# Norm tiles, first memory values and queries in other buffers, a later turn for the third cross head, and whole rows in the last stores

## The chip, the core and the metric

One core of a Trainium2 chip runs the whole program: TensorE (PE) for matrix products, VectorE (DVE), ScalarE (ACT) and GpSimd (POOL) for the elementwise work, SyncE (SP) for issuing most of the transfers. The metric is the device time of one execution in microseconds (us), of which the median over several runs is taken.

## What is computed

One inference step of a two-layer encoder with 1024 features. Its tokens are 256 of a prompt and 32 of a sample, held side by side as 288 columns. Each layer is a mixing attention (another kind in each layer), a cross-attention of 4 heads into 256 memory tokens, and a gated feed-forward net; each of the three has an RMS norm in front and is added to the residual. A last norm gives the output.

```
def rmsnorm(x, g):
    y = xf * lax.rsqrt(jnp.mean(xf * xf, axis=-1, keepdims=True) + RMS_EPS)
    return (y * g)

def memory_attn(h, mk, mv, w_q, w_o):
    q = (h @ w_q).reshape(b, t, XA_HEADS, XA_HEAD_DIM)
    s = jnp.einsum('bqhd,bkhd->bhqk', q, mk) * (XA_HEAD_DIM ** -0.5)
    p = jax.nn.softmax(s, axis=-1)
    o = jnp.einsum('bhqk,bkhd->bqhd', p, mv)
    return o.reshape(b, t, D_MODEL) @ w_o
...
xp = xp + o @ w_out            # mixing
xp = xp + memory_attn(rmsnorm(xp, g_xattn), mk, mv, w_xq, w_xo)
xp = xp + swiglu(rmsnorm(xp, g_ffn), w_gate, w_up, w_down)
...
y_prompt = rmsnorm(xp, g_final); y_sample = rmsnorm(xs, g_final)
```

## The kernel before

**Matrix products.** The residual lies transposed in eight blocks `x[0..7]` of 128 features by 288 tokens. Every product with a weight is made in three terms: operand and weight are each split into a rounded part and a rest (`hh`, `hl` of the activations, `hi`, `lo` of the weights), and PE multiplies hh by hi, hl by hi and hh by lo. A **unit** (L185) is one weight tile of 128 x 1024 (512 KB): SP issues its load into `st`, ACT casts `hi` from it (L162), DVE subtracts to get `lo` (L163), and PE takes 24 matmuls of 288 columns over it, eight blocks of three. `project` (L200) is one unit, after which `tick` (L239) lets each running attention do one step; an attention that says `wait(n)` sits out n units. So the matmuls of the attentions stand in a row between units of weights, in an order that the program fixes.

**Split and norm of the next stage.** At the end of a mixing attention `out_project` adds each finished block `op` to `x[m]` (L399, DVE) and hands it to `Next`, which makes `hh` (L327, ACT) and `hl` (L330, DVE: scale and subtract) and gives the block to `Norm.add`: ACT squares it (`sq`, L269), and the squares are summed (`ssq`): the second by DVE (L280), the third to seventh by POOL, the eighth by DVE (both L282). `Norm.wide` then splits the sum into `qh` (ACT, L403) and `ql` (DVE, L404), PE takes the mean with two matmuls `nrm`, and eight DVE operations (L286 to L294) turn it into `rstd`. These two `nrm` matmuls stand 27 matmuls behind the first `pj` of the queries' projection, which uses the unscaled `hh` and `hl`; `rstd` is multiplied in afterwards (L715, with the sample's part in L717).

**Buffers.** `tok` tiles (66 of them, tag "t") hold nearly everything of one block: `hh`, `hl`, `sq`, `ssq`, the attention outputs `oh` and `ol`. Other tiles are `wk` tags: "w" (8 tiles), "w2" (4 tiles three times as wide), "bi" and "vn" (5 each). A tile that is allocated takes a buffer that was freed, and its first writer waits for the last users of that buffer. The engine waits in its own queue, so all that stands behind it waits too.

**Cross-attention.** `head(hd)` takes the scores `xs`, the softmax on DVE and ACT (`st` the row maxima and sums, `xe` the exponentials; L443 scales `xe` by 1/sum), waits a unit, transposes (`xt`, four plain float32 matmuls, L731), splits into `xw`, waits a unit, and multiplies by the memory values `vh`, `vl` into `xo`. The memory's last values are made in between by `memory.steps` (`mv`, then `vl` by POOL, and POOL's stores of `mv`). `sample` does the same for the 32 sample tokens (`xss`, `xst`, `xso`, `xsp`). PSUM has 4 banks "pj" for units and 4 banks "at" for attentions.

**End.** The last norm's mean is taken by 12 small matmuls, 8 DVE operations on six columns follow, PE transposes the scaled residual, and DVE and ACT scale it out of PSUM into `yo` (L1132, L1134). The sample's 32 rows are transposed as four strips of 256 columns, so that they lie in 128 partitions. SP issues four stores: the sample in blocks 4 x 32 x 256 (128 KB), the first 128 rows in two halves (256 KB each, rows of 2 KB) and the next 128 rows (512 KB, rows of 4 KB).

Of the kernel before, what the change touches and what calls it, by code (L numbers as in the profile page):

```python
# [15 lines left out]
P = 128  # L16
NT = 288
# [9 lines left out]
def encoder_step(ctx: ExitStack, tc: tile.TileContext, a):  # L27
# [17 lines left out]
    def name(s):  # L45
        cnt[0] += 1
        return f"{s}{cnt[0]}"

    def tok(s, dt=F32):
        return tk.tile([P, 320], dt, tag="t", name=name(s))[:, 0:NT]  # L50

    def work(s):
        return wk.tile([P, 512], F32, tag="w", name=name(s))

    def work2(s, dt=F32):
        return wk.tile([P, 768], dt, tag="w2", bufs=4, name=name(s))
# [120 lines left out]
    def together(ins):  # L177

        tc.keep_in_program_order(ins)
# [79 lines left out]
    class Norm:  # L259

        def __init__(self, n=NT, hurry=False):
            self.n, self.acc, self.parts, self.hurry = n, [None, None], 0, hurry
            self.tiles = [0, 128] + ([n - 128] if n > 256 else [])

        def add(self, xb, eng=None):
            q = tok("sq")
            S.activation(q[:, :self.n], xb[:, :self.n], AF.Square)  # L269
            self.parts += 1  # L270
            eng = eng or (V if self.parts == KT else G)
            i = int(self.parts == KT and self.hurry)
            if self.acc[i] is None:
                self.acc[i] = q
                return
            s = tok("ssq")
            b, c = self.acc[i][:, :self.n], q[:, :self.n]
            if self.parts == 2:

                V.scalar_tensor_tensor(s[:, :self.n], b, EPS * KT, c, op0=ALU.add, op1=ALU.add)  # L280
            else:
                eng.tensor_tensor(s[:, :self.n], b, c, ALU.add)  # L282
            self.acc[i] = s
# [11 lines left out]

        def wide(self):

            hi, lo = split(self.acc[0], tok("qh", F32R), tok("ql", F32R), V)
            p = att("nrm")[:, :self.n]
            mm(p, meanr, hi, True, False)  # L300
            mm(p, meanr, lo, False, True)
            r = big.tile([P, NT], F32, tag="rstd", bufs=2, name=name("rstd"))
            self.rsqrt(p, tok("y"), tok("nt"), r)
            return r

        def columns(self, between=None, bank=att):
# [26 lines left out]
    class Next:  # L333


        def __init__(self, gi):
            self.gi, self.norm, self.h, self.waiting = gi, Norm(hurry=gi == 8), ([], []), []

        def block(self, m, start=False):
            g = gain[:, self.gi * KT + m:self.gi * KT + m + 1]  # L340
# [61 lines left out]
    def split(t, hi, lo, eng=G):  # L402
        S.copy(hi, t)  # L403
        eng.tensor_tensor(lo, t, hi.bitcast(F32), ALU.subtract)  # L404
        return hi, lo
# [217 lines left out]
    class Memory:  # L623
# [31 lines left out]
        def step(self):  # L655
            i, l = self.i, self.l
            self.i += 1
            if i < 8:
                p = project(a["w_xk"][l, i], self.h, NP)
                t = tok("mk")  # L660
                V.tensor_tensor(t[:, 0:NP], p[:, 0:NP], memrow, ALU.mult)
                store(a["mkT"][l, i], t[:, 0:NP])
                self.k.append(split(t[:, 0:NP], tok("kh", F32R)[:, 0:NP], tok("kl", F32R)[:, 0:NP]))
            else:

                i -= 8
                heads, n, u, last = (2, 2, i, 3) if i < 4 else (1, 4, i % 2, 1)
                if u == 0:
                    self.p = [acc("mv") for _ in range(heads)]
                w = unit(a["w_xv"][l, i])  # L670
                m = 256 * heads
                for c in range(n):
                    k = n * u + c
                    b = slice(c * m, c * m + m)
                    for t in range(2):
                        d, tb = self.p[t][:, 0:m] if heads == 2 else self.p[0][:, 256 * t:256 * t + 256], slice(128 * t, 128 * t + 128)
                        first = k == 0 and (heads == 2 or t == 0)
                        mm(d, self.h[0][k][:, tb], w[0][:, b], first, False)
                        mm(d, self.h[0][k][:, tb], w[1][:, b], False, False)
                        mm(d, self.h[1][k][:, tb], w[0][:, b], False, k == KT - 1)  # L680
                    if c == 1 and fine[0]:
                        tick(0.5)
                tick(0.5 if fine[0] else 1)
                if u == last:
                    for hd in range(heads):
                        for t in range(2):
                            d = self.p[t][:, 256 * hd:256 * hd + 256] if heads == 2 else self.p[0][:, 256 * t:256 * t + 256]
                            f = hd if heads == 2 else i // 2
                            v = tok("mv")
                            V.tensor_scalar(v[:, 0:NP], d, memcol[:, t:t + 1], None, op0=ALU.mult)  # L690
                            store(a["mv"][l, t, :, f * 256:f * 256 + 256], v[:, 0:NP])
                            self.v[t, f] = split(v[:, 0:NP], tok("vh", F32R)[:, 0:NP], tok("vl", F32R)[:, 0:NP], V if f == 3 else G)


    def cross(layer, cur, memory, nxt):
# [8 lines left out]

        def room(s, i):

            if i < 10:
                return wk.tile([P, NP], F32R, tag=("vn", "bi")[i % 2], bufs=5, name=name(s))
            if i % 2 == 0:
                room.pair = wk.tile([P, 2 * NP], F32R, tag="w2", bufs=4, name=name(s))  # L710
            return room.pair[:, (i % 2) * NP:(i % 2) * NP + NP]

        def evac(b, p):
            t = tok("xq")[:, 0:NP]
# [4 lines left out]
        def head(hd):  # L719
            yield 1  # L720
            s = att("xs")
            for t in range(2):
                for f in range(2):
                    mm3s(s[:, 256 * t:256 * t + 256], q[2 * hd + f], slice(128 * t, 128 * t + 128), memory.k[2 * hd + f], slice(0, NP), f == 0, f == 1)
            e = work("xe")
            softmax(s, [(0, 256), (256, 512)], None, e)
            yield from wait(1)
            tt = att("xt")
            for kt in range(2):
                for t in (1, 0):  # L730
                    i = T.transpose(tt[:, 256 * kt + 128 * t:256 * kt + 128 * t + 128], e[:, 256 * t + 128 * kt:256 * t + 128 * kt + 128], ident)  # L731
                    together(i)
            w = [wk.tile([P, 512], F32R, tag="w", name=name("xw")) for _ in range(2)]
            split_o(tt, w[0], w[1])
            yield from wait(1)
            po = att("xo")
            for f in range(2):
                for kt in range(2):
                    mm3s(po[:, 256 * f:256 * f + 256], memory.v[kt, hd], slice(128 * f, 128 * f + 128), w, slice(256 * kt, 256 * kt + 256), kt == 0, kt == 1)
            for f in range(2):  # L740
                split_o(po[:, 256 * f:256 * f + 256], o[0][2 * hd + f][:, 0:256], o[1][2 * hd + f][:, 0:256])
# [364 lines left out]
        cur = nxt  # L1106


    banks = [[acc("yt"), acc("yt")], [acc("yt"), acc("yt")]]
    strips = att("yt")  # L1110

    def turn(t, m):

        if t < 2:
            return T.transpose(banks[t][m // 4][:, P * (m % 4):P * (m % 4) + P], cur.h[0][m][:, P * t:P * t + P], ident)
        out = strips[NS * (m // 2):NS * (m // 2) + NS, P * (m % 2):P * (m % 2) + P]
        return mm(out, cur.h[0][m][:, P * t:NT], ident)

    def turn_early():
        for m in range(4):  # L1120
            turn(0, m)

    y = cur.norm.columns(turn_early)
    for t, m in [(2, m) for m in range(KT)] + [(0, m) for m in range(4, KT)] + [(1, m) for m in range(KT)]:
        not_before(turn(t, m), cur.norm.summed.ins)
    out = [wp.tile([P, 1024], F32, tag="st", bufs=4, name=name("yo")) for _ in range(3)]

    def read(eng, t, c0, c1):
        src, scale = (banks[t][c0 // 512] if t < 2 else strips), y[:, 2 * t:2 * t + 1]
        b = slice(c0 % 512, c0 % 512 + c1 - c0)  # L1130
        if eng is V:
            together(V.tensor_scalar(out[t][:, c0:c1], src[:, b], scale, None, op0=ALU.mult))  # L1132
        else:
            together(S.activation(out[t][:, c0:c1], src[:, b], AF.Copy, scale=scale))  # L1134


    read(V, 2, 0, 256)
    together(DMA.dma_start(a["y"][2 * P:NT].rearrange("q (s c) -> s q c", s=4), out[2][:, 0:256]))
    read(S, 0, 0, 256)
    read(V, 0, 256, 512)  # L1140
    together(DMA.dma_start(a["y"][0:P, 0:512], out[0][:, 0:512]))
    read(S, 0, 512, 768)
    read(V, 0, 768, 1024)
    together(DMA.dma_start(a["y"][0:P, 512:1024], out[0][:, 512:1024]))
    read(S, 1, 0, 512)
    read(V, 1, 512, 1024)
    together(DMA.dma_start(a["y"][P:2 * P], out[1]))


_OUTS = {  # L1150
# [80 lines left out]
```

## Time and profile before

| what | value |
|---|---|
| median of 3 runs | 946.23 us (946.20 to 946.56) |
| the profiled execution, its own time | 946.38 us |
| its span, first to last instruction | 944.7 us (1.7 us lie around it) |
| mean granted TensorE clock | 0.999 |
| PE, DVE, ACT, POOL busy | 98%, 63%, 51%, 24% of the span |
| chain of work that ended last, by engine | PE 95%, DVE 2%, ACT 1%, DMA 1% |
| one ACT cast `hi`, one DVE subtraction `lo` (means) | 1.050 us, 1.230 us |

The page gives the busy time of each engine, groups of instructions with the mean duration of one, and the chain of work that ended last. Behind it lie views of the trace: the waits of one engine, and the instructions of an engine in order of time, each with its start, its duration and what ended the idle time before it. A PE row's duration includes filling the array and writing out; consecutive matmuls overlap, so for PE the distance from start to start is what counts.

### The profile page before, as it was taken

The numbers are of one execution on the slowest core, as the hardware profiler recorded it, in microseconds if no ns is written. First come the engines' busy times: TensorE is split into PE (matmuls) and PEld (weight loads), VectorE is DVE, ScalarE is ACT, GpSimd is POOL, SyncE is SP. The second block draws the span as 40 slices with busy tenths as digits, with TensorE's granted clock in tenths as the row PEclk, the third lists the DMA queues.
The fourth block names the chain that finished last, engine by engine and source line by source line (L and its number), as shares of the span: only waits on it lengthen the run. The fifth ranks groups of instructions, "written<-read, shape, count | busy, mean of one in ns | idle before, by whom it ended". The sixth has DMA issues, their size and how long they took to land.

```text
span 944.7 us, 18787 instructions
## 1 busy us (share of the span) xinstructions
PE 930.4 (98%) x7350; PEld 899.2 (95%) x7350; DVE 599.1 (63%) x1145; ACT 485.9 (51%) x861; POOL 229.2 (24%) x347
## 2 busy tenths in 40 slices
PE   8999999999999999999999999999999999999996
PEld 8999999999999999999999999899999999999996
DVE  6795555886775555855486666668768655555442
ACT  6566876555554444444455555555546544444330
POOL 4341212201122222400026443322101322221010
PEclk9999999999999999999999999999999999999999
DMA  8675444553444544554556455444425544444431
GB/s 292 198 246 187 164 147 161 175 172 130 147 165 169 175 161 170 184 195 166 183 199 213 170 196 180 172 170 155 146 102 178 179 169 167 166 169 168 167 113 51
DMA packets 49629, 160.96 MB, mean 170 GB/s; under 512 B 7196, under 2 KB 8412, under 8 KB 49540
## 3 DMA queue, kind: packets, MB, share of 16 engines
q1 hardware_dynamic: 45348, 149.23, 46.3%
q0 software_dynamic: 3904, 10.04, 2.9%
q8 instruction: 58, 0.95, 0.4%
q10 hardware_dynamic: 288, 0.48, 0.2%
q14 instruction: 31, 0.25, 0.1%
HBM read 149.58 MB, written 10.15 MB: 169 GB/s over the span
## 4 chain that ended last, share of the span: by engine, by line
PE 95%; DVE 2%; ACT 1%; DMA 1%; issue 0%; POOL 0%; SPq 0%; DVEq 0%; ACTq 0%
PE pj L68 54%; PE dn L68 15%; PE op L68 10%; PE mv L68 5%; PE po L68 1%; PE sc L68 1%; PE zb L68 1%; PE xo L68 1%; PE xs L68 1%; DMA first<-w_first 1%; PE nrm L68 0%; PE xt L731 0%; PE xss L68 0%; PE os L68 0%; POOL ssq L282 0%
## 5 line engine op out<-in xcount | busy, mean ns | idle before, releaser
L162 ACT CAST hi<-st 128x1024 fp32r<-128x1024 f32 x257 | 268.9, 1050 | 287.7 <-issue 104.5
L68 PE MATMUL pj<-hh,hi 128*128 128x288 f32 (+1 forms) x1344 | 397.1, 295 | 0.0
L68 PE MATMUL pj<-hh,lo 128*128 128x288 f32 (+1 forms) x1344 | 394.1, 293 | 0.2 <-DVE lo L163 0.2
L68 PE MATMUL pj<-hl,hi 128*128 128x288 f32 (+1 forms) x1344 | 393.9, 293 | 0.0
L163 DVE TENSOR_TENSOR lo<-st,hi 128x1024 fp32r<-128x1024 f32 x257 | 316.0, 1230 | 80.2 <-PE dn L68 40.1
L68 PEld LDWEIGHTS pj<-hh,hi 128*128 128x128 f32 x1344 | 252.9, 188 | 5.3 <-issue 4.3
L68 PEld LDWEIGHTS pj<-hh,lo 128*128 128x128 f32 x1344 | 252.8, 188 | 0.6 <-DVE lo L163 0.6
L68 PEld LDWEIGHTS pj<-hl,hi 128*128 128x128 f32 x1344 | 252.9, 188 | 0.0
L68 PE MATMUL dn<-fh,hi 128*128 128x288 f32 x416 | 109.9, 294 | 0.0
L68 PE MATMUL dn<-fh,lo 128*128 128x288 f32 x352 | 103.4, 294 | 0.0
L68 PE MATMUL dn<-fl,hi 128*128 128x288 f32 x288 | 84.6, 294 | 0.0
L282 POOL TENSOR_TENSOR ssq<-ssq,sq 128x288 f32<-128x288 f32 (+1 forms) x35 | 37.3, 1066 | 185.7 <-ACT sq L269 151.1
L68 PE MATMUL op<-oh,hi 128*128 128x288 f32 x256 | 76.0, 298 | 0.0
L68 PE MATMUL op<-ol,hi 128*128 128x288 f32 x256 | 75.4, 295 | 0.0
L68 PE MATMUL op<-oh,lo 128*128 128x288 f32 x256 | 75.3, 295 | 0.0
L68 PEld LDWEIGHTS dn<-fh,hi 128*128 128x128 f32 x416 | 74.5, 188 | 0.0
L68 PEld LDWEIGHTS dn<-fh,lo 128*128 128x128 f32 x352 | 66.0, 188 | 0.0
L820 POOL TENSOR_TENSOR fl<-us,fh 128x288 fp32r<-128x288 f32 x36 | 33.2, 922 | 106.1 <-ACT fh L819 106.1
L816 POOL TENSOR_TENSOR gs<-gs,sg 128x288 f32<-128x288 f32 x44 | 39.3, 892 | 74.0 <-ACT sg L814 72.8
L815 DVE TENSOR_TENSOR us<-pj,rstd 128x288 f32<-128x288 f32 x44 | 20.1, 457 | 58.0 <-PE pj L68 58.0
L68 PEld LDWEIGHTS dn<-fl,hi 128*128 128x128 f32 x288 | 54.0, 188 | 0.0
L68 PEld LDWEIGHTS op<-oh,hi 128*128 128x128 f32 x256 | 47.9, 188 | 0.6
(282 smaller groups left out, 1215.8 us busy)
## 6 DMA issues: line engine op xcount, KB each, us to landing
st<-w_gate SPq DMA_DIRECT2D x44, 512.0 KB, 3.2
st<-w_up SPq DMA_DIRECT2D x44, 512.0 KB, 3.3
st<-w_down SPq DMA_DIRECT2D x44, 512.0 KB, 3.2
st<-w_c SPq DMA_DIRECT2D x24, 512.0 KB, 3.5
st<-w_ab SPq DMA_DIRECT2D x21, 512.0 KB, 4.3
st<-w_xk SPq DMA_DIRECT2D x16, 512.0 KB, 3.5
st<-w_xv SPq DMA_DIRECT2D x16, 512.0 KB, 3.3
st<-w_xq SPq DMA_DIRECT2D x16, 512.0 KB, 3.5
```

Source lines behind the costliest of these rows:

```text
L68: return T.matmul(out, lhsT, rhs, start=start, stop=stop, skip_group_check=True)
L162: a = S.copy(hi, st[:, c0:c1])
L163: b = V.tensor_tensor(lo, st[:, c0:c1], hi.bitcast(F32), ALU.subtract)
L282: eng.tensor_tensor(s[:, :self.n], b, c, ALU.add)
L815: V.tensor_tensor(us, pu[:, :NT], cur.r, ALU.mult)
L816: G.tensor_tensor(gs, gs, sg, ALU.mult)
L820: G.tensor_tensor(lo, us, hi.bitcast(F32), ALU.subtract)
```

## The change

It touches five things.

1. The norm in front of each cross-attention (`gi` 2 and 3) takes its tiles `sq`, `ssq`, `qh`, `ql`, `y`, `nt` from tag "w" through a new helper `spare`, where it took `tok` tiles.
2. The memory values `vh`, `vl` of the first head (`f == 0`) go to tag "bi" in place of `tok`.
3. The sixteen query tiles of the cross-attention: the first twelve lie three to a "w2" tile and the last four in "vn"; before, ten lay in "vn" and "bi" in turn and six two to a "w2" tile.
4. The third head (`hd == 2`) waits two units instead of one between its scores and its transposes.
5. At the end the sample's rows are transposed like the others into two banks, each half of a bank pair is read by DVE and ACT, and the stores are two of 256 KB, one of 512 KB and last one of 32 whole rows (128 KB).

```diff
+    def spare(s, dt=F32):
+        return wk.tile([P, NT], dt, tag="w", name=name(s))
...
-        def __init__(self, n=NT, hurry=False):
-            self.n, self.acc, self.parts, self.hurry = n, [None, None], 0, hurry
+        def __init__(self, n=NT, hurry=False, tile=tok):
+            self.n, self.acc, self.parts, self.hurry, self.tile = n, [None, None], 0, hurry, tile
...
-            q = tok("sq")
+            q = self.tile("sq")
...
-            s = tok("ssq")
+            s = self.tile("ssq")
...
-            hi, lo = split(self.acc[0], tok("qh", F32R), tok("ql", F32R), V)
+            hi, lo = split(self.acc[0], self.tile("qh", F32R), self.tile("ql", F32R), V)
...
-            self.rsqrt(p, tok("y"), tok("nt"), r)
+            self.rsqrt(p, self.tile("y"), self.tile("nt"), r)
...
-            self.gi, self.norm, self.h, self.waiting = gi, Norm(hurry=gi == 8), ([], []), []
+            self.gi, self.norm, self.h, self.waiting = gi, Norm(hurry=gi == 8, tile=spare if gi in (2, 3) else tok), ([], []), []
...
-                            self.v[t, f] = split(v[:, 0:NP], tok("vh", F32R)[:, 0:NP], tok("vl", F32R)[:, 0:NP], V if f == 3 else G)
+                            parts = [wk.tile([P, NP], F32R, tag="bi", bufs=5, name=name(s)) if f == 0 else tok(s, F32R)[:, 0:NP] for s in ("vh", "vl")]
+                            self.v[t, f] = split(v[:, 0:NP], *parts, V if f == 3 else G)
...
-            if i < 10:
-                return wk.tile([P, NP], F32R, tag=("vn", "bi")[i % 2], bufs=5, name=name(s))
-            if i % 2 == 0:
-                room.pair = wk.tile([P, 2 * NP], F32R, tag="w2", bufs=4, name=name(s))
-            return room.pair[:, (i % 2) * NP:(i % 2) * NP + NP]
+            if i > 11:
+                return wk.tile([P, NP], F32R, tag="vn", bufs=5, name=name(s))
+            if i % 3 == 0:
+                room.three = wk.tile([P, 3 * NP], F32R, tag="w2", bufs=4, name=name(s))
+            return room.three[:, (i % 3) * NP:(i % 3) * NP + NP]
...
-            yield from wait(1)
+            yield from wait(2 if hd == 2 else 1)
...
-    read(V, 2, 0, 256)
-    together(DMA.dma_start(a["y"][2 * P:NT].rearrange("q (s c) -> s q c", s=4), out[2][:, 0:256]))
-    read(S, 0, 0, 256)
-    read(V, 0, 256, 512)
-    together(DMA.dma_start(a["y"][0:P, 0:512], out[0][:, 0:512]))
-    read(S, 0, 512, 768)
-    read(V, 0, 768, 1024)
-    together(DMA.dma_start(a["y"][0:P, 512:1024], out[0][:, 512:1024]))
-    read(S, 1, 0, 512)
-    read(V, 1, 512, 1024)
-    together(DMA.dma_start(a["y"][P:2 * P], out[1]))
+    for c in (0, 512):
+        read(V, 0, c, c + 256)
+        read(S, 0, c + 256, c + 512)
+        together(DMA.dma_start(a["y"][0:P, c:c + 512], out[0][:, c:c + 512]))
+    for t in (1, 2):
+        read(V, t, 0, 512)
+        read(S, t, 512, 1024)
+        together(DMA.dma_start(a["y"][P * t:min(P * t + P, NT)], out[t][rows[t]]))
```

The order of the instructions on the engines moves with the buffers, since the buffers decide what waits for what. First place: POOL, at the end of layer 0's mixing attention, the five sums `ssq` of the norm. The brackets name the engines that a row waits for. Before:

```order
L282 TENSOR_TENSOR ssq_2276<-ssq_2261,sq_2274 128x288 [waits DVE_49,PE_49,Activation_49]
L282 TENSOR_TENSOR ssq_2316<-ssq_2276,sq_2314 128x288 [waits PE_49,Activation_49]
L282 TENSOR_TENSOR ssq_2356<-ssq_2316,sq_2354 128x288 [waits PE_49,Activation_49]
L282 TENSOR_TENSOR ssq_2396<-ssq_2356,sq_2394 128x288 [waits PE_49,Activation_49,Pool_49]
L282 TENSOR_TENSOR ssq_2436<-ssq_2396,sq_2434 128x288 [waits PE_49,Activation_49,Pool_49]
```

After:

```order
L285 TENSOR_TENSOR ssq_2276<-ssq_2261,sq_2274 128x288 [waits DVE_49,Activation_49]
L285 TENSOR_TENSOR ssq_2316<-ssq_2276,sq_2314 128x288 [waits Activation_49,Pool_49]
L285 TENSOR_TENSOR ssq_2356<-ssq_2316,sq_2354 128x288 [waits Activation_49,Pool_49]
L285 TENSOR_TENSOR ssq_2396<-ssq_2356,sq_2394 128x288 [waits Activation_49,Pool_49]
L285 TENSOR_TENSOR ssq_2436<-ssq_2396,sq_2434 128x288 [waits Activation_49,Pool_49]
```

The sums stand in the same order; none of them waits for PE any more.

Second place: DVE, the last blocks of the same out-projection up to the norm's `ql`. Before:

```order
L163 TENSOR_TENSOR lo_2609<-st_2606,hi_2608 128x1024
L330 SCALAR_TENSOR_TENSOR hl_2351<-x_80,x_78,hh_2350 128x288
L330 SCALAR_TENSOR_TENSOR hl_2391<-x_80,x_78,hh_2390 128x288
L399 TENSOR_TENSOR x_81<-x_81,op_2444 128x288
L330 SCALAR_TENSOR_TENSOR hl_2431<-x_81,x_78,hh_2430 128x288
L163 TENSOR_TENSOR lo_2647<-st_2644,hi_2646 128x1024
L330 SCALAR_TENSOR_TENSOR hl_2471<-x_81,x_78,hh_2470 128x288
L282 TENSOR_TENSOR ssq_2476<-ssq_2436,sq_2474 128x288
L404 TENSOR_TENSOR ql_2554<-ssq_2476,qh_2553 128x288
```

After:

```order
L403 TENSOR_TENSOR x_81<-x_81,op_2404 128x288
L166 TENSOR_TENSOR lo_2607<-st_2604,hi_2606 128x1024
L333 SCALAR_TENSOR_TENSOR hl_2431<-x_81,x_78,hh_2430 128x288
L403 TENSOR_TENSOR x_81<-x_81,op_2444 128x288
L166 TENSOR_TENSOR lo_2643<-st_2640,hi_2642 128x1024
L333 SCALAR_TENSOR_TENSOR hl_2471<-x_81,x_78,hh_2470 128x288
L285 TENSOR_TENSOR ssq_2476<-ssq_2436,sq_2474 128x288
L408 TENSOR_TENSOR ql_2554<-ssq_2476,qh_2553 128x288
```

The rests `hl` of the earlier blocks, three of which stood around the last add to `x`, now stand each behind its own block's add; behind the last add there remain one `lo` and one `hl` ahead of the last sum.

Third place: PE, the third cross head of layer 0. Here `pj` is a unit of the fourth head's queries, `xt` the third head's transposes, `mv` a unit of the memory values. Before:

```order
L68 MATMUL pj_3047<-hh_2242,hi_3043 128x288
L68 MATMUL pj_3047<-hl_2243,hi_3043 128x288
L731 MATMUL xt_3026<-ident,xe_2972 128x128 x4
L68 MATMUL pj_3047<-hh_2242,lo_3044 128x288
L68 MATMUL pj_3047<-hh_2255,hi_3043 128x288
```

After:

```order
L71 MATMUL pj_3032<-hl_2471,hi_3028 128x288
L71 MATMUL pj_3032<-hh_2470,lo_3029 128x288
L736 MATMUL xt_3057<-ident,xe_2965 128x128 x4
L71 MATMUL mv_3081<-hi_3084,hh_690 128x256
L71 MATMUL mv_3081<-lo_3085,hh_690 128x256
```

The transposes moved from the third place of a unit of 24 to behind its last matmul, and the twelve `xo` matmuls that belong to them from in front of the `mv` unit and the eight `xss` to behind these. Two other moves on PE: the second `nrm` matmul stands right behind the first, where three `pj` stood between, and head 0's `xt` right behind the eight `xss`, where four `pj` stood between. Layer 1 has the same moves, and PE's count of instructions is the same.

## Rows read from the trace of the kernel before

**Rows 1.** The page, busy time of each engine (share of the span), instructions

```profile
PE 930.4 (98%) x7350; PEld 899.2 (95%) x7350; DVE 599.1 (63%) x1145; ACT 485.9 (51%) x861; POOL 229.2 (24%) x347
```

**Rows 2.** PE's waits: line, releaser, us in total, times, longest

```profile
PE nrm L68 <- ACT qh L403: 2.5, 2, 1.2
PE xt L731 <- DVE xe L443: 1.9, 2, 1.0
```

**Rows 3.** PE in order of time, layer 0's norm: start, us, instruction, [idle before]

```profile
179.31 0.29 PE L68 MATMUL op<-oh,lo 128*128 128x288 f32 x1
...
182.86 0.30 PE L68 MATMUL pj<-hh,lo 128*128 128x288 f32 x1
184.40 0.40 PE L68 MATMUL nrm<-qh,meanr 128*128 128x288 f32 x1 [1.24 <-ACT qh L403]
```

**Rows 4.** POOL in order of time, the same stretch

```profile
176.85 1.88 POOL L282 TENSOR_TENSOR ssq<-ssq,sq 128x288 f32<-128x288 f32 x1 [6.62 <-PE op L68]
...
181.81 1.39 POOL L282 TENSOR_TENSOR ssq<-ssq,sq 128x288 f32<-128x288 f32 x1 [0.74 <-POOL ssq L282]
```

**Rows 5.** DVE in order of time, the same stretch

```profile
180.33 0.44 DVE L399 TENSOR_TENSOR x<-x,op 128x288 f32<-128x288 f32 x1
...
181.32 1.21 DVE L163 TENSOR_TENSOR lo<-st,hi 128x1024 fp32r<-128x1024 f32 x1
182.45 1.06 DVE L330 SCALAR_TENSOR_TENSOR hl<-x,x,hh 128x288 fp32r<-128x288 f32 x1
183.44 0.45 DVE L282 TENSOR_TENSOR ssq<-ssq,sq 128x288 f32<-128x288 f32 x1
```

**Rows 6.** All `hl` of this shape: count, ns min/median/max, first and last start

```profile
L330 DVE SCALAR_TENSOR_TENSOR hl<-x,x,hh x36: 505/514/1071, 7.6 to 726.4; 128x288 fp32r<-128x288 f32 x36
```

**Rows 7.** DVE in order of time, from the norm's mean to the queries

```profile
185.37 0.46 DVE L286 TENSOR_SCALAR y<-nrm 128x288 int32<-128x288 int32 x1 [0.53 <-PE nrm L68]
...
194.00 0.41 DVE L404 TENSOR_TENSOR ql<-xq,qh 128x256 fp32r<-128x256 f32 x1
```

**Rows 8.** PE in order of time, first head's scores and transposes

```profile
194.47 0.38 PE L68 MATMUL xs<-kh,ql 128*128 128x256 f32 x1
...
198.66 1.06 PE L68 MATMUL xss<-ca,xqs 128*32 128x256 f32 x8
199.65 0.40 PE L68 MATMUL pj<-hh,hi 128*128 128x288 f32 x1
199.89 0.29 PE L68 MATMUL pj<-hl,hi 128*128 128x288 f32 x1
200.02 0.29 PE L68 MATMUL pj<-hh,lo 128*128 128x288 f32 x1
```

**Rows 9.** PE in order of time, third head's transposes

```profile
219.86 0.29 PE L68 MATMUL pj<-hl,hi 128*128 128x288 f32 x1
221.14 0.63 PE L731 MATMUL xt<-ident,xe 128*128 128x128 f32 x4 [0.98 <-DVE xe L443]
```

**Rows 10.** DVE, scaling `xe`: third head, then fourth head

```profile
219.42 1.57 DVE L443 TENSOR_SCALAR xe<-xe,st 128x256 f32<-128x256 f32 x2
...
233.94 0.61 DVE L443 TENSOR_SCALAR xe<-xe,st 128x256 f32<-128x256 f32 x2
```

**Rows 11.** POOL beside the third head's scaling

```profile
218.22 0.59 POOL L249 DMA_DIRECT2D mv<-mv  x1 [35.02 <-DVE mv L690]
...
220.09 0.74 POOL L404 TENSOR_TENSOR vl<-mv,vh 128x256 fp32r<-128x256 f32 x1
```

**Rows 12.** The end, stores issued by SP in order of time

```profile
938.48 0.47 SPq L1141 DMA_DIRECT2D y<-yo  x1
...
939.53 0.51 SPq L1147 DMA_DIRECT2D y<-yo  x1
```

**Rows 13.** DMA from 938.5 to 944.5 us, 40 slices of 0.15: busy tenths, GB/s

```profile
DMA  0000231234779999999999999998422200000000
GB/s 0 0 0 14 41 34 14 68 116 116 171 239 375 396 410 424 396 396 451 410 437 423 437 382 451 410 437 328 164 109 109 109 0 0 0 0 0 0 0 0
```

More of the change, by code (lines that the diff above doesn't have):

```diff
@@ L1106, in encoder_step @@
         cur = nxt
-    banks = [[acc("yt"), acc("yt")], [acc("yt"), acc("yt")]]
-    strips = att("yt")
+    banks = [[acc("yt"), acc("yt")], [acc("yt"), acc("yt")], [att("yt"), att("yt")]]
+    rows = [slice(0, P), slice(0, P), slice(0, NS)]
     def turn(t, m):
[L1114 to L1117, printed above, removed]
+        return T.transpose(banks[t][m // 4][rows[t], P * (m % 4):P * (m % 4) + P], cur.h[0][m][:, P * t:min(P * t + P, NT)], ident)
     def turn_early():
@@ L1123, in encoder_step @@
     y = cur.norm.columns(turn_early)
-    for t, m in [(2, m) for m in range(KT)] + [(0, m) for m in range(4, KT)] + [(1, m) for m in range(KT)]:
-        not_before(turn(t, m), cur.norm.summed.ins)
+    for t in range(3):
+        for m in range(4 if t == 0 else 0, KT):
+            not_before(turn(t, m), cur.norm.summed.ins)
     out = [wp.tile([P, 1024], F32, tag="st", bufs=4, name=name("yo")) for _ in range(3)]
     def read(eng, t, c0, c1):
-        src, scale = (banks[t][c0 // 512] if t < 2 else strips), y[:, 2 * t:2 * t + 1]
+        src, scale, r = banks[t][c0 // 512], y[rows[t], 2 * t:2 * t + 1], rows[t]
         b = slice(c0 % 512, c0 % 512 + c1 - c0)
         if eng is V:
-            together(V.tensor_scalar(out[t][:, c0:c1], src[:, b], scale, None, op0=ALU.mult))
+            together(V.tensor_scalar(out[t][r, c0:c1], src[r, b], scale, None, op0=ALU.mult))
         else:
-            together(S.activation(out[t][:, c0:c1], src[:, b], AF.Copy, scale=scale))
-    read(V, 2, 0, 256)
-    together(DMA.dma_start(a["y"][2 * P:NT].rearrange("q (s c) -> s q c", s=4), out[2][:, 0:256]))
-    read(S, 0, 0, 256)
-    read(V, 0, 256, 512)
-    together(DMA.dma_start(a["y"][0:P, 0:512], out[0][:, 0:512]))
-    read(S, 0, 512, 768)
-    read(V, 0, 768, 1024)
-    together(DMA.dma_start(a["y"][0:P, 512:1024], out[0][:, 512:1024]))
-    read(S, 1, 0, 512)
-    read(V, 1, 512, 1024)
-    together(DMA.dma_start(a["y"][P:2 * P], out[1]))
+            together(S.activation(out[t][r, c0:c1], src[r, b], AF.Copy, scale=scale))
+    for c in (0, 512):
[6 more added lines that the diff above has]
+        together(DMA.dma_start(a["y"][P * t:min(P * t + P, NT)], out[t][rows[t]]))
 _OUTS = {
```

## The prediction

> **What bounds the kernel now.** I read the busy shares first. PE is busy 98% of the span [rows 1], so a change that leaves PE's instructions alone can gain only where PE stands still. I read PE's waits next: in the middle of the program there are two kinds, each once per layer, `nrm` waiting for ACT's `qh` and the third head's `xt` waiting for DVE's `xe` [rows 2]. Then I read PE in order of time around each, for what each costs from start to start. Consecutive `pj` matmuls start 0.13 us apart (199.89 to 200.02) [rows 8]. At the norm 1.54 us lie between two starts (182.86 and 184.40), so 1.41 are lost [rows 3]; at `xt` 1.28, so 1.15 are lost [rows 9]. With the second layer, that is twice 1.41 and twice about 1.13, some 5.1 us, all that the middle of the program offers besides small change. The rest is the end, where the last store decides.
>
> **The norm.** The wait at `nrm` begins far ahead. POOL had stood idle for 6.62 us when it began a sum `ssq` at 176.85, released by PE's `op` matmuls [rows 4]: the tile that it writes was an old attention output, which PE reads to the end of the out-projection. Behind that start three more sums and the squares on ACT follow late, the last POOL sum runs from 181.81 to 183.20, DVE's last sum starts at 183.44 [rows 5], and `nrm` at 184.40, 0.96 later for the sum, `qh` and the hand-overs. With the norm's tiles in "w" the order shows no wait of `ssq` for PE, so POOL's chain comes early, and what is late next is DVE's work on the last block. I add it up from the last `op` matmul, 179.31 plus 0.29: the add to `x` 0.44, one `lo` 1.21 [rows 5], one `hl` 0.51, the usual time [rows 6], and the 0.96 to `nrm`. That gives 182.72. On ACT a cast of 1.05 stands in front of the last `hh`, which is then done near 181.1, before DVE's `lo` ends at 181.25; so ACT is hidden, by 0.15. PE would want `nrm` at 182.99, so by this sum the wait is gone with 0.27 to spare. If the `hl` takes 1.06 instead, as it did beside POOL [rows 5], `nrm` is ready at 183.27 and 0.28 remain. The second `nrm`, now straight behind the first, wants `ql` 0.13 later; DVE makes it while ACT hands over `qh`, some 0.45 after it, so up to 0.2 may remain there. I take 0.1 of waiting per layer, since POOL has no sum left beside that `hl`: gain 1.3 per layer, **2.6**, bounds 2.0 (0.4 left) and 3.0 (also the 0.11 that the first matmul after a stop loses [rows 8]).
>
> **The third head.** DVE's two scalings took 1.57 us together, where the fourth head's take 0.61 [rows 10]; POOL was subtracting `vl` beside them [rows 11], and nothing in the change removes that. The change lets PE do the other unit first: 22 more matmuls at 0.13, 2.9 us, stand in front of `xt`, and the scaling is late by 1.0 only. So the wait goes. What follows moves as well. Between `xt` and `xo` stood 22 matmuls, and no wait shows at `xo`; now 24 `mv` and eight `xss` stand there, so the split into `xw` is covered at least as well. Behind them the third head's output is split while DVE should begin the fourth head's row maxima, and the cover of the fourth `xt` shrinks. No wait shows there now; if it arises, its price is the two subtractions that moved ahead, 0.41 each by the like operation in [rows 7], 0.8 per layer at most. I take nothing. Gain 1.15 and 1.1, **2.25**, bounds 0.7 and 2.4.
>
> **Head 0's transposes.** Small float32 matmuls between units cost a change each way: from the eight `xss` (198.66) to the next `pj` 0.99 pass, and the `pj` behind it follows after 0.24 instead of 0.13 [rows 8]. With `xt` straight behind `xss`, one of the two returns per layer goes. The second `pj` alone shows 0.11; the first start, which I can't split from the eight, may show as much. I take 0.2 per layer, **0.4**, bounds 0 and 0.6. `xe` is wanted 0.5 earlier for it, and it did not wait before; a small wait here is in the lower bound.
>
> **Queries and values in other tiles.** This frees "t" tiles and moves a few DVE operations; no instruction is added, no row of PE waits for these tiles now, and the attentions' loads are long done. I take nothing, bounds minus 0.5 and 0.2.
>
> **The end.** Now the sample's store is issued first and the DMA engines run at 14 to 116 GB/s until about 940; from there some 400 GB/s flow for two and a half microseconds, and the last slices fall off through 164 and 109 [rows 13]. The two 256 KB halves have rows of 2 KB, the last store of 512 KB is issued at 939.53 [rows 12]. After, DVE and ACT read the same bank one behind the other, so the first 256 KB can't go before about 938.35, half a microsecond after the first store now, but 0.1 ahead of the first large one now (938.48); the 512 KB goes near 939.45; the 32 rows last, near 940.0. About 1.18 MB at 410 GB/s take 2.9 us from 939.65 to 939.9, which ends at 942.5 to 942.8, plus a fall-off, against 943.4 to 943.5 now. Nothing shows how 32 rows are spread. If they land as slowly after their issue as the 512 KB do now, 0.5 us are lost; if the queue simply runs full, 0.8 are gained. I take **0.3**. The rows themselves show a store that was not spread: while only the sample's four blocks are out, the engines are busy by one to four tenths [rows 13]. On this the Trainium skill has a rule ("DMA: Bandwidth & Descriptors", section "Why a DMA increments its semaphore by 16 and not by 1"): a transfer uses the largest number of engines up to 16 that divides the sizes of its slowest dimension. By it four blocks get 4 engines, and 32 rows get 16, so the end would come out nearer to the 0.8; the two to four tenths agree with 4 of 16, and no run here shows the 32 rows yet.
>
> **Sum.** 2.6 + 2.25 + 0.4 + 0.3 = 5.55 from the profiled execution's own 946.38 gives 940.8; the median of the runs lies 0.15 lower, so I forecast 940.7. With the bounds of its terms this case reaches from 939.4 (all high, 3.0 + 2.4 + 0.6 + 0.2 + 0.8) to 943 or so (2.0 + 1.6 + 0 + 0 - 0.3).
>
> **Rivals.** *The norm's wait stays.* DVE is the next in line; if it reaches the last add late by one more block's `lo` and `hl` (1.21 + 0.51), `nrm` is ready at 184.44 and nothing is won there. Against it: per block DVE has 0.44 + 1.21 + 0.51 = 2.2 us of work, and PE takes 3.15 (24 x 0.13). For it: the table of instructions puts `lo` ahead of each `hl`. Time 946.23 - 2.95 = 943.3.
>
> *The time is given back a little later.* The first head's `xs` reaches a matmul at 194.47 [rows 8] for which `ql` was done at 194.41 [rows 7]: 0.06 to spare. The sums and the mean come earlier by as much as PE does, the second `nrm` another 0.4, and one `lo` of DVE's chain goes behind the queries. If that `lo` is run anyway, or the fourth head waits, 0.4 to 0.8 per layer come back: 942.0.
>
> *The third head's wait has another cause* that moves along, such as a bank or a "w" tile that its later turn holds: the 2.25 stay, 943.0.
>
> *Slower.* The eight operations for `rstd` at 185.37 and on, 0.46 each, run alone, POOL being idle for 35 us up to 218.22 [rows 11]. Were POOL's sums to fall beside them and stretch each as `hl` was stretched, from 0.51 to 1.06, they would take 4.4 us more, `xs` would wait 3.8 per layer, and the time would be 946.2 - 5.6 + 7.6 = 948.2. It turns into a loss when each takes over 0.88 (2.8 per layer plus the 0.6 of cover, over eight). Against it: the sums now wait for nothing late and come early; and the stretching is not general, since a `lo` beside POOL's sum of 181.81 kept its 1.21 [rows 4, 5]. The Trainium skill ("GPSIMD Engine Reference", "Key points") says that POOL shares its SBUF interfaces with DVE, with contention for DVE instructions in a two-port mode or with two SBUF inputs. `hl` agrees, the `lo`, which has two such inputs as well, does not, so the rule by itself doesn't move my chance.
>
> **Chances.** Forecast 0.62; norm's wait stays 0.12; given back 0.10; third head's stays 0.06; two of these together, or something that no row shows, at 944.4 to 947 0.06; slower 0.04. The range 939.7 to 943.3 holds the first four but for their edges, about 0.85. A difference of 0.2% (1.9 us) is about what a measurement of this kernel can tell from none: faster than 944.3 has 0.88, within 0.2% 0.07, slower 0.05.
>
> **What would show it.** Right: PE's waits after show neither `nrm` for `qh` nor `xt` for `xe`; POOL's sums start without a wait for PE, the last one over before 180; `nrm` starts within 0.3 of the `pj` before it; the out-projection and the first query units keep their pitch of 0.13; the last data moves before 943.4 minus what the rest gained. Wrong: a new row in PE's waits, at `nrm` for `ql`, at `xs` for a query tile, at head 0's or the fourth `xt`; a `lo` that PE waits for; or a last store that lands later after its issue than 4 us.

## The result, and the profile after

The changed kernel takes **939.51 us** (median of 4 runs, 939.33 to 939.55) against 946.22 us (946.13 to 946.56) before: a ratio of 0.9928, 95% interval [0.9911, 0.9945], 6.7 us less. I had forecast 940.7 in a range of 939.7 to 943.3: the sign was right, and the gain was larger than the range allowed, by 0.2 us.

PE's waits in the changed kernel (line, releaser, us in total, times, longest). Only the one at the program's start is left; both rows of [rows 2] are gone:

```profile
PE warm L143 <- POOL identb masks.py:199: 2.6, 1, 2.6
```

PE in order of time (start, us, instruction), which answers to [rows 3], [rows 8] and [rows 9]; the last row is the last norm's matmuls:

```profile
179.17 0.29 PE L71 MATMUL op<-oh,lo 128*128 128x288 f32 x1
...
182.72 0.30 PE L71 MATMUL pj<-hh,lo 128*128 128x288 f32 x1
182.86 0.30 PE L71 MATMUL nrm<-qh,meanr 128*128 128x288 f32 x1
182.99 0.30 PE L71 MATMUL nrm<-ql,meanr 128*128 128x288 f32 x1
...
192.33 0.28 PE L71 MATMUL xs<-kl,qh 128*128 128x256 f32 x1
192.45 0.40 PE L71 MATMUL xs<-kh,qh 128*128 128x256 f32 x2
192.69 0.28 PE L71 MATMUL xs<-kl,qh 128*128 128x256 f32 x1
...
196.90 1.06 PE L71 MATMUL xss<-ca,xqs 128*32 128x256 f32 x8
197.90 0.66 PE L736 MATMUL xt<-ident,xe 128*128 128x128 f32 x4
198.31 0.38 PE L71 MATMUL pj<-hh,hi 128*128 128x288 f32 x1
198.53 0.29 PE L71 MATMUL pj<-hl,hi 128*128 128x288 f32 x1
...
220.97 0.29 PE L71 MATMUL pj<-hh,lo 128*128 128x288 f32 x1
221.10 0.60 PE L736 MATMUL xt<-ident,xe 128*128 128x128 f32 x4
...
928.96 0.78 PE L71 MATMUL nrm<-mean,sq 128*128 128x2 f32 x12
```

Both `nrm` start 0.13 us behind the matmul before them, and so does the third head's `xt`. The last row's counterpart before:

```profile
934.80 0.78 PE L68 MATMUL nrm<-mean,sq 128*128 128x2 f32 x12
```

Laying the same instructions of both kernels beside each other tells where the time went. At the last `op` of layer 0 the changed kernel is 0.14 ahead (179.31, 179.17), at the first `nrm` 1.54 (184.40, 182.86), at head 0's `xss` 1.76 (198.66, 196.90), at the fourth head's `xt` 2.98 (235.04, 232.06), at the last norm 5.84 (934.80, 928.96). So each layer gives about 2.9 us, and the end, the rest of the 6.9 by which the span fell (944.7 to 937.8), gives 1.06.

POOL at the end of layer 0's out-projection, which answers to [rows 4]:

```profile
175.05 0.81 POOL L285 TENSOR_TENSOR ssq<-ssq,sq 128x288 f32<-128x288 f32 x1 [1.00 <-ACT sq L272]
178.22 0.81 POOL L285 TENSOR_TENSOR ssq<-ssq,sq 128x288 f32<-128x288 f32 x1 [2.36 <-ACT sq L272]
```

POOL waits for the squares alone, and its last sum is over at 179.03, before the last `x` is there. DVE from that `x` on, which answers to [rows 5], and its scaling for the third head, which answers to [rows 10]:

```profile
179.50 0.45 DVE L403 TENSOR_TENSOR x<-x,op 128x288 f32<-128x288 f32 x1 [1.14 <-PE op L71]
179.87 1.22 DVE L166 TENSOR_TENSOR lo<-st,hi 128x1024 fp32r<-128x1024 f32 x1
181.01 0.51 DVE L333 SCALAR_TENSOR_TENSOR hl<-x,x,hh 128x288 fp32r<-128x288 f32 x1
181.44 0.45 DVE L285 TENSOR_TENSOR ssq<-ssq,sq 128x288 f32<-128x288 f32 x1
182.38 0.46 DVE L408 TENSOR_TENSOR ql<-ssq,qh 128x288 fp32r<-128x288 f32 x1 [0.50 <-ACT qh L407]
...
217.55 1.60 DVE L447 TENSOR_SCALAR xe<-xe,st 128x256 f32<-128x256 f32 x2
```

The DVE chain is the one that the prediction added up, `qh` is ready near 182.35, and the scaling is as slow as it was, 1.60 us for two.

At the end, first DMA from 932.6 to 938.6 us in 40 slices of 0.15 (busy tenths, GB/s, packets), which answers to [rows 13]:

```profile
DMA  0000089999999999999999892000000000000000
GB/s 0 0 0 0 14 355 423 382 437 410 410 396 382 533 410 410 437 437 437 437 382 410 301 382 82 0 0 0 0 0 0 0 0 0 0 0 0 0 0 0
DMA packets 480, 1.18 MB, mean 197 GB/s; under 512 B 64, under 2 KB 64, under 8 KB 480
...
y<-yo SPq DMA_DIRECT2D x2, 256.0 KB, 2.3
```

and, for the last two rows, the counterparts of the kernel before:

```profile
DMA packets 564, 1.18 MB, mean 197 GB/s; under 512 B 52, under 2 KB 180, under 8 KB 564
...
y<-yo SPq DMA_DIRECT2D x2, 256.0 KB, 3.4
```

The ramp from 14 to 375 GB/s over more than a microsecond and the fall-off through 164 and 109 are gone; the flow goes from 14 to 355 GB/s in one slice and ends as sharply. A store of 256 KB lands 2.3 us after its issue instead of 3.4. I come back to the packets under 512 B below.

### The profile page after: what moved, and what is told of

It reads as the page before. It is cut to its first block, busy times and chain, and to the rows that moved or that the text cites. A ratio compares the mean times of both kernels' runs of the same rounds, so it can differ in the third digit from the quotient of the medians.

```text
span 937.8 us, 18749 instructions
## 1 busy us (share of the span) xinstructions
PE 929.5 (99%) x7342; PEld 899.4 (96%) x7342; DVE 599.7 (64%) x1145; ACT 485.6 (52%) x862; POOL 225.2 (24%) x347
## 4 chain that ended last, share of the span: by engine, by line
PE 98%; DMA 1%; DVE 0%; ACT 0%; ACTq 0%; SPq 0%; issue 0%
PE pj L71 56%; PE dn L71 15%; PE op L71 11%; PE mv L71 5%; PE po L71 1%; PE xo L71 1%; PE xs L71 1%; PE sc L71 1%; PE zb L71 1%; DMA first<-w_first 1%; PE xt L736 0%; PE xss L71 0%; PE os L71 0%; PE nrm L71 0%; PE zs L71 0%; PE vt L423 0%
```

## The experiments

### Each part alone

The end alone, on the kernel before (the diff is the last piece of the change):

> The kernel before with the new end alone (whole rows, sample last). By the prediction's term 0.3 us less than before, 945.9, and within 0.8 less and 0.5 more. By the trace of the changed kernel, where the time from the last norm matmuls to the last landing is 7.89 instead of 8.97 us, 1.1 us less: 945.1, with PE's waits at the norm and at the third head as before.

It takes 945.38 us against 946.24, 0.86 less, ratio 0.9991 [0.9981, 1.0000]. The interval just reaches 1, but the slowest of its ten runs (945.48) is faster than the fastest of the 21 of the kernel before (946.11). In the trace the span falls by 1.1 (943.6). PE's waits at `nrm` and `xt` are as before. So the end was worth three times what I took for it.

The norm's tiles alone:

```diff
+        ... Norm(hurry=gi == 8, tile=spare if gi in (2, 3) else tok) ...
```

> The kernel before with the norm's tiles alone in the other tag. By the prediction the whole gain at the norm comes from this edit: 2.6 to 3.2 us less, 943.0 to 943.6, no row for nrm in PE's waits, xt still there with 1.9. Rival: the activations' own tiles hh and hl of the last blocks still come from the t ring and wait for the last output block's matmuls, so ACT and DVE stay late and nrm keeps a wait of 0.5 or more per layer: 945 to 946.

942.83 us, 3.41 less, 0.9964 [0.9951, 0.9977]. The row for `nrm` is gone. The `hh` and `hl` of the last blocks do still come from the "t" ring (the order shows ACT's and DVE's waits for PE there), but they are soon through. DVE's rows in that run:

```profile
178.59 0.81 DVE L333 SCALAR_TENSOR_TENSOR hl<-x,x,hh 128x288 fp32r<-128x288 f32 x1 [0.17 <-ACT hh L330]
179.55 0.46 DVE L402 TENSOR_TENSOR x<-x,op 128x288 f32<-128x288 f32 x1 [0.16 <-PE op L71]
```

DVE is ready for the last `x` again 0.16 before PE's last `op` releases it. The rival falls.

The third head's later turn alone:

```diff
-            yield from wait(1)
+            yield from wait(2 if hd == 2 else 1)
```

> The kernel before with the third head's later turn alone. By the prediction 2.25 us less, 943.9 to 944.0: no row for xt in PE's waits, nrm still there with 2.5, scaling of xe still 1.5 to 1.6 us for two. Rival: the wait moves to the fourth head's xt or to xo and 0.4 to 0.8 per layer come back, 944.8 to 945.6.

943.98 us, 2.26 less, 0.9976 [0.9966, 0.9985]. The row for `xt` is gone, `nrm` still has 2.5, no new row arises. The end, the norm's tiles and the third head, each alone, add up to 6.53 of the 6.7 of the full change.

The queries' and the first values' tiles alone, an edit that I had put at nothing:

> The kernel before with the queries' and the first memory values' tiles alone moved. By the prediction nothing: 946.2, and PE's wait at nrm stays at 2.5. Rival: the t tiles that it frees are enough by themselves, since only the last two of POOL's sums then wait for the last output block: nrm's wait goes, 2.6 to 3.2 us less, 943.0 to 943.6.

942.90 us, 3.34 less, 0.9964 [0.9950, 0.9978]: **as much as the norm's tiles.** The row for `nrm` is gone here too. POOL in this run:

```profile
171.67 2.11 POOL L282 TENSOR_TENSOR ssq<-ssq,sq 128x288 f32<-128x288 f32 x2 [1.78 <-ACT sq L269]
176.50 1.88 POOL L282 TENSOR_TENSOR ssq<-ssq,sq 128x288 f32<-128x288 f32 x1 [2.72 <-PE op L68]
178.94 0.81 POOL L282 TENSOR_TENSOR ssq<-ssq,sq 128x288 f32<-128x288 f32 x1 [0.56 <-ACT sq L269]
```

POOL still waits for PE's `op`, until nearly the same time as before (176.50, in [rows 4] 176.85), and the released sum still takes 1.88. But from that point on only two sums are left, where there were four, and the last ends at 179.75 in place of 183.20.

### How many sums stand behind the wait

To see whether it is the number of sums, the queries' tiles and only half of the value tiles were moved (the line in which it differs from the run with all four):

```diff
+    parts = [wk.tile([P, NP], F32R, tag="bi", ...) if f == 0 and t == 0 else tok(s, F32R)[:, 0:NP] for s in ("vh", "vl")]
```

> The kernel before with the queries' tiles moved and only two of the four value tiles (one of the two token halves) in the other tag, so half as many t tiles come free. The last three of POOL's sums still wait for the last output block, four before, two with all tiles moved. If the wait at nrm hangs on how many sums stand behind that point, at some 0.9 us each: 0 to 0.5 left per layer, 942.9 to 943.9. If it is all or nothing, as long as one sum waits early enough: 946.2.

943.80 us, 2.5 less, 0.9974 [0.9963, 0.9984]; some 1.0 of it is a wait at `xt` that went in one layer, as told below. PE's waits at `nrm`:

```profile
PE nrm L68 <- ACT qh L403: 0.6, 2, 0.3
```

PE's two `nrm` rows in layer 0:

```profile
183.46 0.40 PE L68 MATMUL nrm<-qh,meanr 128*128 128x288 f32 x1 [0.32 <-ACT qh L403]
183.95 0.40 PE L68 MATMUL nrm<-ql,meanr 128*128 128x288 f32 x1
```

and POOL's sums ahead of them:

```profile
176.83 1.88 POOL L282 TENSOR_TENSOR ssq<-ssq,sq 128x288 f32<-128x288 f32 x1 [4.07 <-PE op L68]
179.27 1.79 POOL L282 TENSOR_TENSOR ssq<-ssq,sq 128x288 f32<-128x288 f32 x2 [0.55 <-ACT sq L269]
```

Three sums stand behind the wait, the last done at 181.06, and `nrm` starts 0.62 behind the matmul before it (182.84). So with four, three and two sums the excess over 0.13 is 1.41, 0.49 and 0: the wait at `nrm` goes with the number of late blocks. (There the second `nrm` waits as well, 0.49 from start to start, since it stands right behind the first.)

But it is not the end of POOL's queue that sets `nrm`. DVE's rows in this run:

```profile
180.31 0.44 DVE L399 TENSOR_TENSOR x<-x,op 128x288 f32<-128x288 f32 x1
...
182.49 0.44 DVE L282 TENSOR_TENSOR ssq<-ssq,sq 128x288 f32<-128x288 f32 x1
```

DVE's last sum starts 1.43 behind the end of POOL's last one, so it waits for something else: DVE's own chain, which begins with an `x` at 180.31 (179.50 in the changed kernel). The chain followed back from `nrm` in the kernel before shows how that `x` comes late (start, us, what):

```profile
176.85 1.89 POOL ssq L282
...
179.12 0.53 ACT hh L327
...
179.67 0.74 DVE hl L330
180.41 0.36 DVE x L399
180.77 0.62 DVE hl L330
181.39 1.11 DVE lo L163
...
183.44 0.46 DVE ssq L282
...
183.91 0.44 ACT qh L403
184.40 0.40 PE nrm L68
```

Only the first of POOL's late sums is in it. Behind it ACT's next square and `hh` come late, then DVE's `hl` of the earlier blocks, and these stand in front of the last `x`. Against the changed kernel DVE's last sum is 2.0 late (183.44, 181.44): `x` 0.83, one more `hl` behind it 0.62, and 0.56 by which the last `hl` is stretched beside POOL [rows 4, 5]. With three sums behind the wait the extra `hl` and the stretch of the last one are gone, `x` is still 0.81 late, and `lo` takes 0.24 longer; with two, DVE is ready for the last `x` before PE's `op` releases it.

### Each of the two left out of the full change

> The changed kernel with the norm's tiles back in the t ring; the queries' and values' tiles stay moved. If freeing t tiles by the values is enough by itself, as the run with the tiles alone showed, nothing is lost: 939.3 to 939.8 and no row for nrm. If the two edits only work together in the full change: 2.5 to 3 us more, 942.0 to 942.5.

939.57 us (0.9929 [0.9914, 0.9943]).

> The changed kernel with the queries' and first values' tiles put back; the norm's tiles stay moved. If either edit does: 939.3 to 939.9. If the values' tiles were what mattered in the full change: 942.0 to 942.5.

939.64 us (0.9930 [0.9915, 0.9944]). Neither is missed by more than 0.13 us, which these runs can't tell from nothing. The two edits are two cures for one wait; in the full change one of them is spare.

### What stretches the scaling of `xe`

The kernel before, with the third head's two `vl` subtractions on DVE; POOL keeps its two issues of stores there:

```diff
-    ..., V if f == 3 else G)
+    ..., V if f >= 2 else G)
```

> The kernel before with the third head's vl subtractions on DVE instead of POOL; POOL still issues the stores of mv there. If the subtraction on POOL is what stretches DVE's scaling of xe (1.57 us for two): 0.6 to 0.7 for two, xt reached late by 0.3 to 0.5 instead of 1.15, 944.6 to 945.2. If POOL's issuing of the store stretches it, which begins ahead of the second scaling: still 1.2 us or more for two, and the time 946 or above, as vl now stands on DVE too.

944.21 us, 2.1 less, 0.9978 [0.9969, 0.9987]. DVE and POOL in this run:

```profile
219.30 0.62 DVE L443 TENSOR_SCALAR xe<-xe,st 128x256 f32<-128x256 f32 x2
...
219.49 0.54 POOL L249 DMA_DIRECT2D mv<-mv  x1 [0.81 <-DVE st L441]
```

The scalings take 0.62 with a store being issued beside them, so the issue is not the cause and the subtraction is. How the subtraction takes hold the rows don't show: before, the first scaling takes 0.35 and the second, begun near 219.7, takes 1.30, while by its own row the subtraction begins at 220.09 [rows 11], when 0.35 would just be over. `xt` is no longer late enough to show in PE's waits, which is more than I expected of it. The run with two value tiles says the same without an edit: in its layer 1 POOL's subtraction happened to start at 680.24, just after the scalings (679.49, 0.62 us), and there `xt` shows no wait, while in its layer 0 the two met, 1.57 us, and it did. The Trainium skill ("GPSIMD Engine Reference", "Key points") names contention between POOL and DVE for DVE instructions in a two-port mode or with two SBUF inputs. The scaling has one tensor input, so by that rule it runs in a two-port mode; no run here shows the mode, only the 1.57 and the 0.62.

### The end: place or shape of the sample's store

The kernel before, its sample store moved from first to last; then the same bytes as four stores of 32 rows of 1 KB, also last:

```diff
-    together(DMA.dma_start(a["y"][2 * P:NT].rearrange("q (s c) -> s q c", s=4), out[2][:, 0:256]))
     ...
     together(DMA.dma_start(a["y"][P:2 * P], out[1]))
+    together(DMA.dma_start(a["y"][2 * P:NT].rearrange("q (s c) -> s q c", s=4), out[2][:, 0:256]))
```

```diff
+    for s in range(4):
+        together(DMA.dma_start(a["y"][2 * P:NT, 256 * s:256 * s + 256], out[2][NS * s:NS * s + NS, 0:256]))
```

> The kernel before with one thing changed at its end: the sample's store, still in blocks of 4 x 32 x 256, is issued last instead of first. Theory of the shape: this store runs on 4 of the 16 engines, in 128 rows of 1 KB, some 32 of 0.05 us on each; put last, its four engines do them behind their share of the 512 KB, and the last landing moves later by about 1.6 us less the 0.9 us by which the large stores now start earlier: 946.2 to 947.0. Theory of the place: a small store in front only holds the large ones up, and moved behind it costs little: 945.2 to 945.5.

> As the one with the blocks last, but the same 128 KB go as four stores of 32 rows of 1 KB each, each of which may use all 16 engines. Theory of the shape: the four engines are no longer behind, all end together, 945.3 to 945.7 (three more issues of about 0.4 us on SP, partly beside the 512 KB). Theory of the place: the same as with the blocks last, within 0.2.

The blocks last take 947.04 us (0.8 more than before, 1.0008 [0.9999, 1.0017]), the four stores 946.01 (0.25 less, 0.9997 [0.9987, 1.0007]). DMA from 938.5 to 944.5 us, blocks last:

```profile
DMA  0029999999999999999922130302222222210000
GB/s 0 0 96 369 396 382 423 383 423 437 396 519 410 410 437 437 410 382 437 260 27 14 7 14 0 20 0 55 75 96 102 96 96 96 96 48 21 0 0 0
DMA packets 564, 1.18 MB, mean 197 GB/s; under 512 B 52, under 2 KB 180, under 8 KB 564
```

and four stores last:

```profile
DMA  0000499999999999999995935115100000000000
GB/s 0 0 0 0 164 410 396 423 423 410 369 410 410 492 437 410 437 437 410 437 437 205 274 82 137 41 27 164 27 0 0 0 0 0 0 0 0 0 0 0
DMA packets 624, 1.18 MB, mean 197 GB/s; under 512 B 112, under 2 KB 240, under 8 KB 624
```

The shape is what matters. Blocks in last place run alone at 96 GB/s with two tenths of the engines busy, and end about a microsecond after the four stores do; the 947.04 lies 0.04 above what the theory of the shape gave. Two tenths agree with 4 of 16, and the packets under 512 B fit one for each engine that a store uses: four stores left 52 of them in the kernel before and in the one with blocks last, which is 3 x 16 + 4; the changed kernel's four left 64, and the seven stores of the last run 112, each 16 per store. With that the rule on the number of engines from the Trainium skill ("DMA: Bandwidth & Descriptors", "Why a DMA increments its semaphore by 16 and not by 1") is borne out on both sides: four blocks got 4 engines, 32 rows got 16.

I missed the four stores' size: I expected 945.3 to 945.7. SP issued them over 2.23 us, up to 942.02 (0.79 us for one of them), so the last of the four came late. And put first, as before, the blocks do another harm: the 256 KB stores, issued behind them, land 3.4 us after their issue in place of 2.3.

Two things make up that harm, by the trace's records of single packets. In the kernel before four of a large store's sixteen small packets come 0.4 to 0.5 us behind the other twelve (for the 512 KB: twelve from 942.59 to 942.88, four from 943.33 to 943.43); that is the fall-off, and it fits four engines that had the blocks to finish. The ramp is another thing, for it holds up the twelve as well: their packets of the first 256 KB come up to 2.5 us after its issue (940.99, issued at 938.48), where with the four stores last all sixteen have come after 1.6 (939.96, 938.32). With blocks last a slow start comes at their own place, about a microsecond at 0 to 55 GB/s ahead of the 96. Why a store in such blocks starts slowly and holds up the others, no run here shows.

### A version that reads the banks side by side

In the changed kernel DVE and ACT take halves of one bank, one behind the other. Here DVE takes the first bank, ACT the second:

```diff
-    for c in (0, 512):
-        read(V, 0, c, c + 256)
-        read(S, 0, c + 256, c + 512)
-        together(DMA.dma_start(a["y"][0:P, c:c + 512], out[0][:, c:c + 512]))
-    for t in (1, 2):
+    for t in range(3):
         read(V, t, 0, 512)
         read(S, t, 512, 1024)
-        together(DMA.dma_start(a["y"][P * t:min(P * t + P, NT)], out[t][rows[t]]))
+        for c in ((0, 512) if t == 0 else (0,)):
+            e = c + 512 if t == 0 else 1024
+            together(DMA.dma_start(a["y"][P * t:min(P * t + P, NT), c:e], out[t][rows[t], c:e]))
```

> The changed kernel with DVE reading the first bank and ACT the second bank whole, side by side, instead of each bank by halves one behind the other. The first store is issued at 3.2 us after the last norm matmuls instead of 3.5, and the data phase of 3.1 us follows it: 939.2, 0.3 less than the changed kernel. If the store's start hangs on something else: 939.5. If both halves coming at once delay the later stores: up to 939.7.

939.32 us (939.21 to 939.57), 0.9926 [0.9914, 0.9939] against before. SP's first store goes at 932.28, 3.2 behind the last norm's matmuls (929.07); in the changed kernel it is 3.5 (928.96, 932.50):

```profile
932.28 1.82 SPq L1143 DMA_DIRECT2D y<-yo  x4
```

The span is 937.5 instead of 937.8. That is the expected 0.3 in the trace and 0.2 in the medians, but the runs of the two kernels overlap, so a gain is likely and not shown.

## Why the prediction was wrong, point by point

| term | forecast | measured |
|---|---|---|
| norm, both layers | 2.6 (2.0 to 3.0) | 3.41 alone |
| third head, both layers | 2.25 (0.7 to 2.4) | 2.26 alone |
| head 0's transposes | 0.4 (0 to 0.6) | 0.1 in the trace |
| queries' and values' tiles | 0 (-0.5 to 0.2) | 3.34 alone, no difference that shows (0.13) beside the norm's |
| the end | 0.3 (-0.5 to 0.8) | 0.86 alone, 1.06 of the span |

Two terms were too small, by about the same amount: the end (0.9 to 1.06 for 0.3) and the norm (3.4 for 2.6). With either put right alone the forecast, 940.1 or 939.9, would have lain in the range; the two together took the time out of it, although head 0's transposes, 0.3 too large, made up for a part.

**The end is the first step that failed.** I dated the full flow of data, 939.65 to 939.9, by the kernel before, where the large stores start late while the blocks are out; the delay went away with the blocks. I also left a fall-off standing, which was four engines finishing last. Both signs were in the rows that I cited: two tenths busy while the blocks were out, the fall-off at the end. I weighed 0.5 lost and 0.8 gained and took 0.3 as if the two ends of the term were alike. With 0.9 in its place the sum is 940.1.

**The norm is the second: the wait and what frees it were right, its price and its path were not.** That POOL's sums start late for a buffer, what comes next without that (DVE's last block), and that `nrm` is ready by 182.72 are borne out: the trace has `ssq` at 181.44 and `qh` done near 182.35, earlier than my sum, since DVE's operations follow one another faster than their durations add up (0.37 apart for 0.45). So the 0.1 of leftover wait is not there. Beyond that, the wait cost more than its idle time: 0.11 for the restart of PE, which I counted only in the bound, and another 0.12 at `xs`. I read 0.06 to spare there, from the end of `ql` at 194.41 to a matmul at 194.47 [rows 7, 8]. It was a wait too short for the table of waits: that matmul starts 0.15 behind the one before instead of 0.12 and lasts 0.38, and the next follows 0.22 later. At `nrm`, which did wait, the hand-over from the end of `qh` took about as long (0.05 in the chain above), so 0.06 was the hand-over and nothing to spare. After, the same place runs through at 0.12 (192.33, 192.45, then 192.69 behind two). Together 1.41 + 0.11 + 0.12 = 1.64 per layer, 3.3 in both.

The path I had wrong: I let the delay run through POOL's four sums to DVE's last one. POOL's last sum was over at 183.20, while DVE was busy with its `hl` until its last sum began at 183.44; the delay had come by way of ACT and the `hl` of earlier blocks, as told above. And I called the stretching beside POOL not general, since a `lo` beside POOL's sum of 181.81 kept its 1.21. But that sum took 1.39, where two of POOL's rows after show 0.81: there POOL was the one that lost the time.

**The cause at the norm was told too narrowly.** I put the whole gain on the norm's tiles and nothing on the values' tiles. Either does it. I had read in the order that the "t" ring was short, but not that the same shortage can be cured at the other side, by who else takes its tiles. That the 0 for the values' tiles did no harm to the sum was luck: the change holds both cures, and with the values' tiles alone 3.34 would have come where I had forecast nothing.

**The third head was right** in mechanism and size, 2.26 against 2.25, down to the scaling that stays slow; the fourth head's `xt` did not wait, nor did `xo`. That POOL's subtraction does the stretching was argued then and is shown now.

**Head 0's transposes** give 0.05 per layer, not 0.2: in the rows of after the step from the eight `xss` to what follows costs as much when `xt` follows (196.90 to 197.90, 1.00) as it did when `pj` followed (0.99), the step from `xt` to the next `pj` is some 0.06 longer, and of the short restarts behind only one is gone.

**The range.** The sum's own bounds reached down to 939.4, or 939.2 with the 0.15 that the forecast itself takes off, and I cut the range at 939.7. At the other end the 943 is added up with 1.6 for the third head and -0.3 for the end, where the terms' own bounds are 0.7 and -0.5, and without the -0.5 of the tiles. No rival came true. With 0.12 at `xs` and the restarts in the sum, and the end as the experiment measured it, the forecast would have been 946.38 - 3.3 - 2.25 - 0.1 - 0.9 = 939.8 for the profiled execution, which took 939.55.

## What to carry to other kernels

A wait for a buffer costs by what stands behind it, and not only on the engine that waits: follow the chain back from the engine that matters, count the steps that come late on each, and look for any user of the same ring that can move, not only for the one that waits. Before a term is dated by the delays of the kernel as it is, ask whether the change removes the cause of those delays too. And a margin as small as the 0.06 us here between a producer's end and its consumer's start can be a wait: look at the distance to the next start.

## What the runs showed that I had not expected

A store of 128 KB in blocks of 4 x 32 x 256 ran at 96 GB/s by itself, while others at full flow reach some 410; in front of the others it delayed their landing by 1.1 us (3.4 against 2.3). DVE's scaling of 128 x 256, 0.35 us for one, took 1.3 beside POOL's subtraction of 0.74, so it lost more time than the subtraction lasted; POOL's own time there did not move (0.74 to 0.76).
